# Strassen weight sums made together, and one normalised operand moved to another tile, in an encoder trunk

## The chip, the cores and the metric

The kernel runs on one core of a Trainium2 chip. The metric is the time on the device in microseconds (us), lower is better. A time is the median of several executions.

## The reference

One layer of a bidirectional encoder on 16 learned meta tokens and 1024 tokens of width 1024, all in float32: a gated feed-forward layer, a mixer of three attention branches, a second gated feed-forward layer, each after an RMS norm, and a last norm. The change touches the two feed-forward layers:

```python
def rms_norm(x, g):
    xf = x.astype(jnp.float32)
    y = xf * lax.rsqrt(jnp.mean(xf * xf, axis=-1, keepdims=True) + EPS)
    return (y * g.astype(jnp.float32)).astype(x.dtype)

def swiglu(x, w_in, w_out):
    g, u = jnp.split(x @ w_in, 2, axis=-1)
    return (jax.nn.silu(g) * u) @ w_out
...
    h = h + 0.5 * swiglu(rms_norm(h, norm_ffn1[l]), w_ffn1_in[l], w_ffn1_out[l])
    h = h + token_mixer(...)
    h = h + 0.5 * swiglu(rms_norm(h, norm_ffn2[l]), w_ffn2_in[l], w_ffn2_out[l])
    return rms_norm(h, final_norm)[:, N_META:]
```

`w_in` is 1024 x 5632, `w_out` 2816 x 1024.

## The kernel before, in words

**Precision.** A float32 product is made of three TensorE passes. Each operand is split in two parts: ScalarE copies it to a rounded type (`copy_r`, line 96: `wH` of weights, `bh` of activations), VectorE subtracts the copy from the original (`sub`, line 99: `wL`, `bl`), and the passes are H x H, H x L and L x H (lines 495, 496 and 498). `wsplit` (line 114) does it for weights. Its tiles `wH` and `wL` have four buffers, so splits run ahead of the products.

**Strassen stations.** A feed-forward layer runs as `ffn_in` (line 506) and `ffn_out` (line 565), both as loops over *stations*: one station multiplies a 2 x 2 arrangement of weight blocks `a11`, `a12`, `a21`, `a22` with a 2 x 2 arrangement of activation blocks by the seven products of the Strassen-Winograd scheme instead of eight. `ffn_in` has 22 steps `j`: `j` = 0 runs as eight plain products (`plain`, line 441), the other 21 as stations. `ffn_out` has 12 stations. With two layers that is 66 stations.

`station` (line 461) loads the four weight blocks into two tiles, `ra` (`a11` and `a12`) and `rb` (`a21` and `a22`), each with one buffer (line 433, DMAs of line 438 on SP's queue), and makes sums of them on GpSimd: `s1` = `a21` + `a22` (line 469), `s2` = `s1` - `a11` (line 470), and `a11` - `a21`, written over `a21` (line 471). The fourth sum, `a12` - `s2`, is made inside `mats`: after product 2's split of `s2` it is written over `s2` (line 477). `products` (line 481) asks `mats` for one split after the other, in the order of `CHAIN` (line 354): products 0, 1, 2, 4, 3, 6, 5. Product 6 takes the fourth sum. Each product runs for two blocks of columns, `b` = 0 and 1, into PSUM banks that are taken in turn (`psd`, line 89), and is then added up by VectorE (line 504) or copied by ScalarE.

**Operand builds.** For `ffn_in`, `build_b` (line 377) prepares the seven right-hand operands of a block. Four multiplications each (line 398, VectorE) make `b11`, `b21`, `b12` and `b22`, which are split at once as operands 0, 1, 3 and 6 (`final`, line 387) and used by `j` = 0. Then come four differences `t1` to `t4` (lines 409 to 412; on GpSimd by line 102 in the first layer, on VectorE by line 99 in the second), written over tiles that are no longer needed, and the splits of operands 2, 4 and 5, later of operand 3. `b11`, `b12` and `b21` lie in the tiles `oA`, `oT` and `e` of the block; `b22` and `t1` lie in the two tiles that later hold operand 5 (`slot_tags`, line 357). The tile `e` is also that of `ev` (line 530), the three evacuated pieces of a step. Tile `oA1` is also used for `wt` (line 1422), sums of the second layer's output weights, made on GpSimd by `tsums` (line 369, lines 372 to 375), as are sums of activations (`tsum`, line 627), which go to DRAM by stores of lines 631 to 633.

**What sets the order.** The program is written in one order, and a scheduler of the tile framework orders each engine's queue ahead of time with a timing simulation of its own (`schedule_with_timeline_sim=True`); so an instruction can stand elsewhere in its queue than in the text. On the chip each queue runs in its written order, and an instruction that waits holds up all behind it on its engine. A tile with one buffer is reused when the last reader of its old content is done.

Of the kernel before, what the change touches and what calls it, by code (L numbers as in the profile page):

```python
# [9 lines left out]
F32 = mybir.dt.float32  # L10
F32R = mybir.dt.float32r
AF = mybir.ActivationFunctionType
ALU = mybir.AluOpType

P = 128
# [20 lines left out]
class Trunk:  # L36
# [61 lines left out]
    def sub(self, out, a, b):  # L98
        return self.nc.vector.tensor_tensor(out=out, in0=a, in1=b, op=ALU.subtract)  # L99
# [20 lines left out]

    def dense(self, ps, W, XH, XL, c0, n, nk=KT):
        mm = self.nc.tensor.matmul
        order = self.KORD if nk == KT else range(nk)
        for i, k in enumerate(order):
            H, L = W[k // 4]
            ks = slice(k % 4 * P, (k % 4 + 1) * P)
            mm(ps[:, :n], H[:, ks], XH[k][:, c0:c0 + n], start=(i == 0), stop=False)  # L127
            mm(ps[:, :n], H[:, ks], XL[k][:, c0:c0 + n], start=False, stop=False)  # L128
            mm(ps[:, :n], L[:, ks], XH[k][:, c0:c0 + n], start=False, stop=(i == nk - 1))  # L129
# [3 lines left out]

    def ahead(self, W, col, chunks, tags):

        for (c0, n), tag in zip(chunks, tags):
            self.pre[col, c0] = ps = self.ps(tag)
            self.dense(ps, W, self.uh, self.ul, c0, n)

    def proj(self, box, col, c0, n):  # L140
        ps = self.pre.pop((col, c0), None)
        if ps is None:
            ps = self.dps()
            self.dense(ps, box["W"], self.uh, self.ul, c0, n)
        return ps

    def wfirst(self, col):
        W = self.W0.pop(col, None)
        return self.wcols(self.w_in, col, self.sub_pool) if W is None else W
# [227 lines left out]
    def build_b(self, pool, bt, w, blk, h, gcol, c0, tags, sub, ordered):  # L377


        nc = self.nc  # L380
        n = 4 * w
        b11, b12, b21 = (pool.tile([P, n], F32, tag=tag, name="bu") for tag in tags)
        p5, th, tl = self.slot_tags(pool, blk, 5)
        b22, t1 = (p5.tile([P, n], F32, tag=tag, name="bu") for tag in (th, tl))
        last = []

        def final(i, src):
            bt[blk][i] = HL = self.bslot(pool, blk, i, w)
            return self.split_b(HL, src)

        def norm(q, t, i):
            hs = slice((q % 2) * w, (q % 2) * w + w)
            rs = slice(c0 + hs.start, c0 + hs.stop)

            with self.behind(last[-2] if ordered and len(last) > 1 else None):
                for kk in range(4):
                    k = kk + 4 * (q // 2)
                    nc.vector.scalar_tensor_tensor(
                        out=t[:, kk * w:(kk + 1) * w], in0=h[:, k, hs], scalar=self.gT[:, gcol + k:gcol + k + 1],
                        in1=self.R[:, rs], op0=ALU.mult, op1=ALU.mult)  # L400
            last.append(final(i, t))

        norm(0, b11, 0)
        norm(2, b21, 1)
        yield
        norm(1, b12, 3)
        norm(3, b22, 6)
        t2, t3, t4 = b11, b12, b21
        sub(t1, b12, b11)
        sub(t2, b22, t1)  # L410
        sub(t3, b22, b12)
        sub(t4, b21, t2)
        for i, src in ((2, t2), (4, t1), (5, t4)):
            final(i, src)
        yield
        final(3, t3)
        yield
# [43 lines left out]
    def station(self, pool, srcs, nk=4):  # L461

        nc = self.nc
        n = nk * P
        a11, a12, a21, a22 = self.raws(pool, srcs, n)
        s1 = pool.tile([P, 512], F32, tag="s1", name="s1")[:, :n]
        s2 = pool.tile([P, 512], F32, tag="s2", name="s2")[:, :n]
        tt = nc.gpsimd.tensor_tensor
        tt(out=s1, in0=a21, in1=a22, op=ALU.add)  # L469
        tt(out=s2, in0=s1, in1=a11, op=ALU.subtract)  # L470
        tt(out=a21, in0=a11, in1=a21, op=ALU.subtract)

        def mats(i):
            src = (a11, a12, s2, a21, s1, a22, s2)[i]
            W = self.wsplit(src)
            if i == 2:
                tt(out=s2, in0=a12, in1=s2, op=ALU.subtract)
            return W
        return mats

    def products(self, mats, bts, w, nk, evac, after=None):
# [106 lines left out]
    def ffn1(self, hT):  # L588
# [3 lines left out]
        with tc.tile_pool(name="f1", bufs=1, reuse_waits="tile") as pool:  # L592
# [6 lines left out]
            def block(b, lead):  # L599
                for i in ([] if b else [8]) + list(range(4 * b, 4 * b + 4)):  # L600
                    self.load_x(pool, hT, i)[1]()
                steps = self.build_b(pool, bt, w, b, hT[:, :, 2 * w * b:2 * w * (b + 1)], 0, 2 * w * b,
                                     (f"oA{b}", f"oT{b}", f"e{b}"), self.sub_pool, False)
                next(steps)
                next(steps)
                if b == 0:
                    lead()
                for _ in range(4):
                    yield
                next(steps)  # L610
                yield
# [26 lines left out]
            def after(i):  # L638
                for b in range(2):
                    nxt[b][i] = build(0, b, i, 4)  # L640

            self.ffn_in(pool, a["w_ffn1_in"][0], bt, w, block, emit, after)
            def srcs(c, n, nk):
                rows = w1o[8 * c * P:(8 * c + 2 * nk) * P, :].rearrange("(k i p) d -> i p k d", i=2, p=P)
# [730 lines left out]
    def ffn2(self, hp):  # L1375
# [3 lines left out]
        with tc.tile_pool(name="f2", bufs=1, reuse_waits="tile") as pool:  # L1379
# [6 lines left out]
            def block(b, lead):  # L1386
                if b == 0:
                    lead()
                steps = self.build_b(pool, bt, w, b, hT[:, :, 512 * b:512 * b + 512], 16, NM + 512 * b,
                                     (f"oA{b}", f"oT{b}", f"e{b}"), self.sub, True)  # L1390
                next(steps)
                next(steps)
                yield
                yield
                for f in ([] if b else self.token_half(pool, ssum, 1)):
                    pin = f()
                    yield pin
                if b:
                    yield
                    yield  # L1400
                next(steps)
                yield
# [32 lines left out]
            def after(i):  # L1435
                for b in range(2):
                    nxt[b][i] = build(0, b, i, 4)

            self.ffn_in(pool, a["w_ffn2_in"][0], bt, w, block, emit, after)
            hacc = hp.tile([P, 8, D], F32, tag="h", name="hacc")  # L1440
            for i in range(8):
# [112 lines left out]
```

## Time and profile before

| | before |
|---|---|
| median of 3 executions | 2679.34 us |
| lowest and highest | 2678.97, 2684.99 us |
| the profiled execution | 2684.01 us |
| its span, first to last instruction | 2682.2 us |
| mean granted TensorE clock | 0.987 |
| busy: TensorE, VectorE, ScalarE, GpSimd | 96%, 62%, 48%, 30% |

PE is TensorE's matmuls, PEld its weight loads, DVE VectorE, ACT ScalarE, POOL GpSimd, SP SyncE, which issues DMAs. A `q` after the engine's name marks its sequencer. A row of a timeline has the start, the duration, the engine, the line, the operation, the tiles (out<-in), the shape and the count; in brackets stands how long the engine had been idle before it, and what ended that.

### The profile page before, as it was taken

How to read it: one execution, taken by the hardware profiler on the slowest of the kernel's cores; microseconds unless marked ns; L12 is line 12 of the kernel's file. 1: busy time of each engine (PE TensorE's matmuls, PEld its weight loads, DVE VectorE, ACT ScalarE, POOL GpSimd, SP SyncE). 2: the span in 40 equal slices, each digit the busy share in tenths (PEclk: the TensorE clock that was granted, in tenths of full speed). 3: DMA queues.
4: the chain of work that ended last, by engine and by line, in shares of the span. 5: the costliest groups of instructions: out<-in, count | busy, mean ns of one | idle time of the engine just before them, and what ended most of it. 6: DMA issues, size and time to landing. Idle time of an engine off the chain costs nothing.

```text
span 2682.2 us, 46662 instructions
## 1 busy us (share of the span) xinstructions
PE 2587.5 (96%) x17648; PEld 2384.7 (89%) x17648; DVE 1664.3 (62%) x3569; ACT 1283.5 (48%) x2456; POOL 807.0 (30%) x697
## 2 busy tenths in 40 slices
PE   6999999999999999999999999999999999999998
PEld 5999999899989989999998888788789999998786
DVE  7644455766867767866777444645485444447667
ACT  5433333532446655656677555554344334334333
POOL 5443454523411111122221111004104444443322
PEclk8999999999999999999999999999999999999999
DMA  3244632542431222223322332436434545566433
GB/s 100 78 126 123 201 112 88 208 134 87 162 108 58 73 71 76 54 70 76 79 62 70 94 93 89 133 99 199 131 99 142 171 154 157 182 228 204 157 122 102
DMA packets 366576, 319.90 MB, mean 119 GB/s; under 512 B 33880, under 2 KB 323759, under 8 KB 366350
## 3 DMA queue, kind: packets, MB, share of 16 engines
q1 hardware_dynamic: 357420, 311.96, 37.6%
q10 hardware_dynamic: 8498, 4.21, 0.6%
q8 instruction: 139, 2.28, 0.4%
q0 software_dynamic: 432, 0.74, 0.2%
q14 instruction: 87, 0.71, 0.1%
HBM read 220.39 MB, written 94.78 MB: 118 GB/s over the span
## 4 chain that ended last, share of the span: by engine, by line
PE 76%; DVE 7%; DMA 6%; issue 5%; POOL 3%; ACT 3%; SPq 0%; POOLq 0%; DVEq 0%; ACTq 0%
PE ps_d L127 7%; PE ps_d L128 7%; PE ps_d L129 7%; PE ps_s L495 5%; PE ps_s L496 5%; PE ps_s L498 5%; PE ps_t L495 5%; PE ps_t L496 5%; PE ps_t L498 5%; PE ps_t L854 3%; PE ps_s L842 2%; PE ps_s L843 2%; PE ps_d L495 2%; PE ps_d L496 2%; PE ps_d L498 2%
## 5 line engine op out<-in xcount | busy, mean ns | idle before, releaser
L127 PE MATMUL ps_d<-uh,wH 128*128 128x512 f32 (+2 forms) x1096 | 381.7, 348 | 6.0 <-DVE t L832 3.2
L129 PE MATMUL ps_d<-uh,wL 128*128 128x512 f32 (+2 forms) x1096 | 375.7, 343 | 0.0
L128 PE MATMUL ps_d<-ul,wH 128*128 128x512 f32 (+2 forms) x1096 | 375.6, 343 | 0.0
L495 PE MATMUL ps_s<-bh,wH 128*128 128x260 f32 (+2 forms) x1229 | 328.5, 296 | 14.5 <-ACT wH L96 9.2
L495 PE MATMUL ps_t<-bh,wH 128*128 128x260 f32 (+2 forms) x1225 | 326.3, 295 | 5.8 <-ACT ev L532 2.1
L102 POOL TENSOR_TENSOR wL<-wr,wH 128x512 fp32r<-128x512 f32 x104 | 134.6, 1305 | 641.9 <-ACT wH L96 423.3
L496 PE MATMUL ps_s<-bl,wH 128*128 128x260 f32 (+2 forms) x1229 | 326.7, 294 | 0.0
L496 PE MATMUL ps_t<-bl,wH 128*128 128x260 f32 (+2 forms) x1225 | 325.3, 294 | 0.0
L469 POOL TENSOR_TENSOR s<-rb 128x512 f32<-128x512 f32 (+1 forms) x66 | 91.6, 1388 | 622.6 <-DMA rb<-in_w_ffn_in_dram 275.2
L495 PEld LDWEIGHTS ps_s<-bh,wH 128*128 128x128 f32 x1229 | 232.6, 189 | 24.6 <-ACT wH L96 10.9
L495 PEld LDWEIGHTS ps_t<-bh,wH 128*128 128x128 f32 x1225 | 232.7, 190 | 14.8 <-ACT wH L96 4.1
L99 DVE TENSOR_TENSOR pL<-ps_t,pH 128x256 fp32r<-128x256 f32 (+2 forms) x264 | 151.9, 582 | 140.5 <-ACT pH L96 130.6
L496 PEld LDWEIGHTS ps_s<-bl,wH 128*128 128x128 f32 x1229 | 232.8, 189 | 6.0 <-issue 0.9
L496 PEld LDWEIGHTS ps_t<-bl,wH 128*128 128x128 f32 x1225 | 232.4, 190 | 5.9 <-issue 0.9
L127 PEld LDWEIGHTS ps_d<-uh,wH 128*128 128x128 f32 x1096 | 207.2, 189 | 30.4 <-DVE t L832 4.4
L96 ACT ACTIVATE wH<-s 128x512 fp32r<-128x512 f32 (+1 forms) x198 | 120.7, 616 | 231.5 <-POOL s L470 102.3
L129 PEld LDWEIGHTS ps_d<-uh,wL 128*128 128x128 f32 x1096 | 207.3, 189 | 23.3
L128 PEld LDWEIGHTS ps_d<-ul,wH 128*128 128x128 f32 x1096 | 207.4, 189 | 19.7
L99 DVE TENSOR_TENSOR wL<-s,wH 128x512 fp32r<-128x512 f32 (+1 forms) x198 | 171.2, 866 | 76.4 <-ACT wH L96 75.9
L498 PE MATMUL ps_s<-bh,wL 128*128 128x260 f32 (+2 forms) x1229 | 212.4, 294 | 0.0
L498 PE MATMUL ps_t<-bh,wL 128*128 128x260 f32 (+2 forms) x1225 | 210.9, 293 | 1.3 <-DVE wL L99 1.3
L96 ACT ACTIVATE pH<-ps_t 128x256 fp32r<-128x256 f32 (+2 forms) x264 | 130.1, 508 | 124.2 <-PE ps_o L938 34.5
(372 smaller groups left out, 6614.9 us busy)
## 6 DMA issues: line engine op xcount, KB each, us to landing
ra<-in_w_ffn_in_dram SPq DMA_DIRECT2D x88, 256.0 KB
rb<-in_w_ffn_in_dram SPq DMA_DIRECT2D x88, 256.0 KB
bl<-optd SPq DMA_DIRECT2D x35, 512.0 KB
wr<-in_w_in_dram SPq DMA_DIRECT2D x30, 512.0 KB
bl<-opd SPq DMA_DIRECT2D x28, 520.0 KB
q<-q SPq DMA_DIRECT2D x48, 256.0 KB
wr<-in_w_gate_dram SPq DMA_DIRECT2D x24, 512.0 KB
gd<-t SPq DMA_DIRECT2D x48, 256.0 KB
```

What stands on the lines that cost most here:

```text
L96: self.nc.scalar.activation(out, in_, AF.Copy, scale=scale)
L99: return self.nc.vector.tensor_tensor(out=out, in0=a, in1=b, op=ALU.subtract)
L102: self.nc.gpsimd.tensor_tensor(out=out, in0=a, in1=b, op=ALU.subtract)
L127: mm(ps[:, :n], H[:, ks], XH[k][:, c0:c0 + n], start=(i == 0), stop=False)
L128: mm(ps[:, :n], H[:, ks], XL[k][:, c0:c0 + n], start=False, stop=False)
L129: mm(ps[:, :n], L[:, ks], XH[k][:, c0:c0 + n], start=False, stop=(i == nk - 1))
L469: tt(out=s1, in0=a21, in1=a22, op=ALU.add)
L495: mm(ps, H[:, ks], bH[:, cs], start=(begins and x == 0), stop=False, skip_group_check=not begins)
L496: mm(ps, H[:, ks], bL[:, cs], start=False, stop=False, skip_group_check=not begins)
L498: mm(ps, L[:, ks], bH[:, cs], start=False, stop=(x == nk - 1), skip_group_check=not begins)
L842: mm(ps[:, :n], T[:, s, 0, qs], k[:, ks:ks + n], start=True, stop=False)
L854: nc.tensor.transpose(pt[:rows, i * P:(i + 1) * P], src, self.ident)
```

## The change

The fourth weight sum gets a tile of its own (`s4`, tag `s3`), is made right after `s2`, and `mats` only splits. In `build_b`, `b21` moves from the tile `e` of the block to the first of the two tiles of operand 2; `t4` is made before `t3`, and operand 2 is split after 4 and 5. The tile `e` thereby holds only `ev` (and in the second layer `res` of the output projection), three quarters of its former size.

```diff
@@ build_b
-        b11, b12, b21 = (pool.tile([P, n], F32, tag=tag, name="bu") for tag in tags)
+        b11, b12 = (pool.tile([P, n], F32, tag=tag, name="bu") for tag in tags)
         p5, th, tl = self.slot_tags(pool, blk, 5)
         b22, t1 = (p5.tile([P, n], F32, tag=tag, name="bu") for tag in (th, tl))
+        p2, th, _ = self.slot_tags(pool, blk, 2)
+        b21 = p2.tile([P, n], F32, tag=th, name="bu")
...
         sub(t1, b12, b11)
         sub(t2, b22, t1)
+        sub(t4, b21, t2)
         sub(t3, b22, b12)
-        sub(t4, b21, t2)
-        for i, src in ((2, t2), (4, t1), (5, t4)):
+        for i, src in ((4, t1), (5, t4), (2, t2)):
             final(i, src)
@@ station
         tt = nc.gpsimd.tensor_tensor
+        s4 = pool.tile([P, 512], F32, tag="s3", name="s4")[:, :n]
         tt(out=s1, in0=a21, in1=a22, op=ALU.add)
         tt(out=s2, in0=s1, in1=a11, op=ALU.subtract)
+        tt(out=s4, in0=a12, in1=s2, op=ALU.subtract)
         tt(out=a21, in0=a11, in1=a21, op=ALU.subtract)
 
         def mats(i):
-            src = (a11, a12, s2, a21, s1, a22, s2)[i]
-            W = self.wsplit(src)
-            if i == 2:
-                tt(out=s2, in0=a12, in1=s2, op=ALU.subtract)
-            return W
+            return self.wsplit((a11, a12, s2, a21, s1, a22, s4)[i])
         return mats
@@ both calls of build_b (ffn1 and ffn2)
-                                     (f"oA{b}", f"oT{b}", f"e{b}"), ...
+                                     (f"oA{b}", f"oT{b}"), ...
```

## Rows read from the trace of the kernel before

**Rows 1.** The page, part 1: busy us, share of the span, instructions.
```profile
PE 2587.5 (96%) x17648; PEld 2384.7 (89%) x17648; DVE 1664.3 (62%) x3569; ACT 1283.5 (48%) x2456; POOL 807.0 (30%) x697
```
**Rows 2.** Stretches: us, busy us (count) per engine, granted clock, DMA share, GB/s.
```profile
2030.00:2380.00 350.00, 350.00 (x2960) 350.00 (x2959) 169.54 (x294) 138.21 (x275) 147.35 (x136) 1.00 0.52 161
...
526.80:532.10 5.30, 0.18 (x2) 0.00 (x0) 5.30 (x7) 4.02 (x5) 2.87 (x2) 0.73 0.57 176
532.10:536.00 3.90, 3.90 (x18) 3.90 (x19) 2.97 (x6) 0.02 (x1) 0.00 (x0) 0.50 0.24 74
```
**Rows 3.** Line 477 in the whole trace: durations, and what ended GpSimd's idle time.
```profile
L477 POOL TENSOR_TENSOR s<-ra,s x66: 1013/1292/1741, 77.4 to 2658.6; 128x512 f32<-128x512 f32 x58, 128x384 f32<-128x384 f32 x8
...
  DVE wL L99: 55.3, 51
```
**Rows 4.** Timeline of GpSimd, 510 to 531 us.
```profile
517.40 2.28 POOL L471 TENSOR_TENSOR rb<-ra,rb 128x512 f32<-128x512 f32 x1
...
521.69 1.20 POOL L375 TENSOR_TENSOR tsum<-act,tsum 128x260 f32<-128x260 f32 x1
...
526.25 1.72 POOL L477 TENSOR_TENSOR s<-ra,s 128x512 f32<-128x512 f32 x1
```
**Rows 5.** Timeline of SP's queue, 516 to 531 us.
```profile
522.91 0.36 SPq L633 DMA_DIRECT2D opd<-tsum  x1
527.99 0.93 SPq L438 DMA_DIRECT2D ra<-in_w_ffn_out_dram  x2
```
**Rows 6.** Timeline of ScalarE, 520 to 533 us.
```profile
528.00 0.63 ACT L96 ACTIVATE wH<-s 128x512 fp32r<-128x512 f32 x1 [5.00 <-POOL s L477]
...
531.44 0.61 ACT L96 ACTIVATE wH<-ra 128x512 fp32r<-128x512 f32 x1
```
**Rows 7.** Timeline of TensorE, 526 to 536 us.
```profile
532.11 0.58 PE L495 MATMUL ps_s<-bh,wH 128*128 128x260 f32 x1 [5.12 <-ACT wH L96]
```
**Rows 8.** Timeline of TensorE, 2018 to 2022 us.
```profile
2021.54 0.39 PE L495 MATMUL ps_t<-bh,wH 128*128 128x256 f32 x1 [2.12 <-ACT ev L532]
```
**Rows 9.** Timeline of ScalarE, 2014 to 2022 us.
```profile
2020.58 0.63 ACT L96 ACTIVATE wH<-s 128x512 fp32r<-128x512 f32 x1 [5.13 <-POOL s L477]
2021.12 0.36 ACT L532 ACTIVATE ev<-ps_t 128x256 f32<-128x256 f32 x1
```
**Rows 10.** Timeline of GpSimd, 2011 to 2024 us.
```profile
2014.04 4.60 POOL L372 TENSOR_TENSOR wt<-wo 128x256 f32<-128x256 f32 x1 [20.53 <-DVE bl L99]
...
2019.29 1.26 POOL L477 TENSOR_TENSOR s<-ra,s 128x512 f32<-128x512 f32 x1
```
**Rows 11.** Timelines of ScalarE, 2449 to 2456 and 2536 to 2541 us.
```profile
2451.32 0.63 ACT L96 ACTIVATE wH<-s 128x512 fp32r<-128x512 f32 x1 [0.36 <-POOL s L477]
...
2538.72 1.06 ACT L96 ACTIVATE bh<-bl 128x1024 fp32r<-128x1024 f32 x1 [0.42 <-DMA bl<-optd]
```
**Rows 12.** Timelines of TensorE around 2455, 2540 and 2619 us.
```profile
2455.89 0.50 PE L495 MATMUL ps_s<-bh,wH 128*128 128x512 f32 x1 [1.71 <-ACT wH L96]
...
2540.35 0.79 PE L495 MATMUL ps_d<-bh,wH 128*128 128x512 f32 x1 [3.66 <-ACT wH L96]
...
2619.40 0.51 PE L495 MATMUL ps_s<-bh,wH 128*128 128x512 f32 x1 [1.03 <-ACT wH L96]
```
**Rows 13.** Timeline of GpSimd, 2605 to 2616 us.
```profile
2613.29 1.02 POOL L477 TENSOR_TENSOR s<-ra,s 128x384 f32<-128x384 f32 x1 [3.29 <-ACT bh L96]
```
**Rows 14.** Timelines of GpSimd, 24 to 46 and 56 to 73 us.
```profile
37.03 1.30 POOL L471 TENSOR_TENSOR rb<-ra,rb 128x512 f32<-128x512 f32 x1
...
56.54 16.02 POOL L102 TENSOR_TENSOR bu<-bu 128x1040 f32<-128x1040 f32 x4 [2.82 <-issue]
```
**Rows 15.** Timeline of VectorE, 61 to 76 us.
```profile
64.43 5.86 DVE L99 TENSOR_TENSOR bl<-bu,bh 128x1040 fp32r<-128x1040 f32 x2 [3.42 <-ACT bh L96]
70.21 2.90 DVE L99 TENSOR_TENSOR wL<-ra,wH 128x512 fp32r<-128x512 f32 x1
```
**Rows 16.** Timeline of TensorE, 72 to 75 us.
```profile
73.16 0.75 PE L498 MATMUL ps_t<-bh,wL 128*128 128x260 f32 x4 [1.31 <-DVE wL L99]
```

More of the change, by code (lines that the diff above doesn't have):

```diff
@@ L602, in block @@
                 steps = self.build_b(pool, bt, w, b, hT[:, :, 2 * w * b:2 * w * (b + 1)], 0, 2 * w * b,
-                                     (f"oA{b}", f"oT{b}", f"e{b}"), self.sub_pool, False)
+                                     (f"oA{b}", f"oT{b}"), self.sub_pool, False)
                 next(steps)
@@ L1389, in block @@
                 steps = self.build_b(pool, bt, w, b, hT[:, :, 512 * b:512 * b + 512], 16, NM + 512 * b,
-                                     (f"oA{b}", f"oT{b}", f"e{b}"), self.sub, True)
+                                     (f"oA{b}", f"oT{b}"), self.sub, True)
                 next(steps)
```

## The prediction

> **What bounds the kernel now.** I read the busy shares first. TensorE is busy for 96% of the span, every other engine for 62% or less [rows 1], so a change outside TensorE can only win what TensorE spends idle or at a low clock. The table of stretches then shows where there is nothing to win: from 2030 to 2380 us, some eighteen stations of the second `ffn_in`, TensorE is busy for 350.00 of 350.00 us with 2960 matmuls, 0.118 us each, at full clock [rows 2]. The same table shows a hole at the change from the first `ffn_in` to `ffn_out`: 5.3 us almost empty, then 3.90 us at a granted clock of 0.50, the lower of TensorE's two levels, 1.2 GHz, in which 18 matmuls take 0.217 us each [rows 2].
>
> Next I asked for line 477, the fourth sum. It runs 66 times, once per station, 1.29 us in the median, and GpSimd stood idle 55.3 us in 51 of these for VectorE's `wL` of product 2 [rows 3]: the old sum overwrites the tile that this split reads. That idle time is GpSimd's and costs nothing by itself. So the question is at which stations a late line 477 reaches TensorE. Going through TensorE's gaps and what ended them, I find five places, all at the edges of the stages, and the startup.
>
> **Part 1: the fourth sum moves ahead of `mats`.** Nothing is added or removed: 66 sums of 1.29 us before and after. Moved are the sum itself, the release of `ra` (line 477 was the last reader of `a12`), the DMAs of the next `ra` on SP, and the sixth split on ScalarE. The new last reader of `ra` among the sums is line 471, which now runs one sum later.
>
> *End of the first `ffn_in` (place 1).* Line 471 ended at 517.40 + 2.28 = 519.68, then came `tsums`, then line 477 from 526.25 to 527.97 [rows 4]. SP issued the `ra` loads at 527.99, behind an `opd<-tsum` store of 522.91 [rows 5]. ScalarE waited 5.00 us for line 477 and split the new `ra` at 531.44 [rows 6]; TensorE, idle for 5.12 us, went on at 532.11 [rows 7]. After the change line 471 ends 1.72 later (line 477's time here), at 521.40. If the store still stands in front, it waits for line 375, which ended at 521.69 + 1.20 = 522.89 and now ends at 524.61; with 0.36 for its issue, `ra` goes out near 525.0, its split follows 531.44 - 527.99 = 3.45 later at 528.4, the matmul 0.67 after that at 529.1. Gain 3.0. The shorter hole also gives back part of the slow stretch, which lost 3.90 x (1 - 0.118/0.217) = 1.8 us; I take 0.5. Sum 3.5; the ends are 0 (another wait takes over at once) and 5.12 + 1.8 = 6.9. Next in line is VectorE, busy with operand splits there.
>
> *First station of the second `ffn_in` (place 2).* A matmul waited 2.12 us [rows 8] for the silu of line 532, which stood on ScalarE right behind a `wH<-s` that had waited 5.13 us for line 477 [rows 9]. Line 477 stood on GpSimd behind a `wt` sum of 4.60 us which itself waited for a VectorE split [rows 10]. With the sum made early this whole chain falls away: 2.1; ends 0 and 2.1.
>
> *Later edges (places 3 to 5).* At 2455.89 TensorE had waited 1.71 us for a split of `ra`, but ScalarE had no gap before it except 0.36 us for line 477: 0.4, ends 0 and 1.7 [rows 11, 12]. At 2540.35 it had waited 3.66 us; on ScalarE the gap that this could close is 0.42 us, a wait for operands: 0.4, ends 0 and 3.7 [rows 11, 12]. At 2619.40 it had waited 1.03 us; there line 477 stood idle 3.29 us, more than the whole stall: 1.0, ends 0 and 1.0 [rows 12, 13].
>
> *At nothing.* Line 471 itself comes a sum later in all stations. It feeds the fifth product, and in the full stretch TensorE never waits [rows 2]; without that cover it would cost 1.29 us a station. `tsums` behind it are later or earlier by a sum; only stores wait for them.
>
> **Part 2: `b21` in product 2's tile.** No instruction is added. `e0` and `e1` shrink by a quarter, which pays for the new tile. A wait goes: the first `ev` of a block shared its tile with `b21`, so line 532 had to follow product 5's split; I count no gain for it. A wait comes: product 2's copy may only start when product 5's split has read `t4`, so its split is now the last but one of a block. Behind it on ScalarE and VectorE stand the first weight splits. In block 1 of the first `ffn_in` four GpSimd sums take 16.02 us [rows 14]; VectorE's two operand subtracts behind them take 5.86, then the first `wL` 2.90 [rows 15], and TensorE waited 1.31 us for that `wL` [rows 16]. With product 2's subtract gone from in front of it, `wL` can start up to 2.93 earlier and the 1.31 vanish. Against that, the fourth weight sum now enters GpSimd's queue early, beside line 471 at 37.03 [rows 14], among the sums and small powers on which the startup hangs: 1.30 at that row's time. These two cancel: 0; the ends are a gain of 1.3 and a loss of 1.30 + 2.93 = 4.2. In the second `ffn_in`, the `wt` sum waits for product 2's split of block 1 and starts later; behind it there stands line 477 no more, and its results only go to a store.
>
> **A rule against it.** Line 471 took 2.28 us at place 1, where VectorE was full of operand splits [rows 4], and 1.30 at 37.03 [rows 14]; so GpSimd and VectorE do hold each other up. The Trainium skill, GPSIMD Engine Reference, section 1 (Specifications), says that GpSimd's SBUF interfaces are shared with VectorE and contend with VectorE instructions that have two SBUF inputs. By that rule the sum, pushed into the stretch full of splits, would hold VectorE for as long as it runs. In the rows' terms that is 1.72 us lost at place 1 [rows 4]: 1.8 left there, 5.7 in all, 2673.6. That time lies inside the forecast's own band; I give it 0.10 of the 0.45 below, since the same sum ran in the same stretch before, only 9 us later.
>
> **Sum.** 3.5 + 2.1 + 0.4 + 0.4 + 1.0 + 0 = 7.4 us. The profiled execution took 2684.01 us, 1.8 more than its span of 2682.2, and lies 4.7 above the median 2679.34; against it the sum gives 2676.6, against the median 2671.9. I forecast **2672 us**. All upper ends (6.9 + 2.1 + 1.7 + 3.7 + 1.0 + 1.3 = 16.7) give 2662.6, no gain and the lower end of the start give 2683.5.
>
> **Rivals.**
> *The next wait takes over.* At place 1 VectorE, at places 3 and 4 ScalarE's queue keeps TensorE waiting; or the order written into the queues puts the new sum behind `tsums` again, so that it isn't made early where it matters. For it: ScalarE's missing gaps at place 3. Against it: place 2 has a clear chain with idle ScalarE. Only about 2 us are left: 2677. Chance 0.23.
> *More than the sum.* `ra` goes out ahead of the store, the clock stays up through place 1, and the start wins 1.3: 6.9 + 2.1 + 0.4 + 0.4 + 1.0 + 1.3 = 12.1, 2667. For it: line 471 ends before that store. Chance 0.14.
> *Slower: product 2's operand comes late.* Place: the four block builds, where the copy into the shared tile waits for product 5's subtract and ScalarE's queue stands behind it. Price: one stretched subtract, 2.93 us [rows 15], each time it isn't covered; with three of four uncovered and the stations' gains lost, 2679.3 + 8.8 = 2688. It decides if TensorE reaches the third product before that split, so if the idle time before 92 us and between 2012 and 2030 us grows by over 5. Against it: the third product comes two products, some 5.7 us at 24 x 0.118 each, after the first. Chance 0.18, and it reaches from 2681 up.
> *The forecast*, 2667 to 2677: 0.45.
>
> **Numbers.** About 0.3%, 8.0 us, is what a measurement can tell from no change, so faster begins below 2671.3. The forecast lies on that line: a little over half of its 0.45 is below, 0.26, with 0.14 from the larger gain: faster 0.40. The rest, 0.19, with 0.23 and 0.03 of the slower case: same 0.45. Slower 0.15. The range from 2663 to 2685 leaves out most of the slower case above and little below.
>
> **What would show it.** Right: line 477's work stands directly behind line 470's in each station with no idle for `wL`; the hole at 527 to 536 us is half as long; no 5 us wait of ScalarE near 2020; TensorE's total idle is some 7 us less. Wrong: TensorE's wait at these places is as long, with another releaser; or the start up to the first station is longer by several us.

## The result and the profile after

The changed kernel takes 2704.99 us in the median of 4 executions (2701.66 to 2710.63), beside 2679.15 for the kernel before (4 executions now): 1.0087 of it, 95% interval 1.0071 to 1.0104. It is slower, by 23 us by that ratio and by 26 in the medians, where the prediction had 2672, and lies outside the predicted range. The profiled execution took 2701.66 us, its span is 2699.8.

The page's first part, kernel after:

```profile
PE 2593.9 (96%) x17648; PEld 2387.4 (88%) x17648; DVE 1665.7 (62%) x3569; ACT 1282.2 (47%) x2456; POOL 815.6 (30%) x697
```

Counts are those of [rows 1], shares lie within a point: no engine has more to do, so I look for gaps. Stretches of after, columns as in [rows 2]:

```profile
526.80:532.10 5.30, 5.26 (x44) 5.26 (x45) 5.30 (x7) 3.88 (x5) 5.30 (x5) 1.00 0.70 227
532.10:536.00 3.90, 2.61 (x22) 2.44 (x21) 3.90 (x5) 0.63 (x1) 0.22 (x1) 1.00 0.40 137
2030.00:2380.00 350.00, 340.96 (x2860) 338.90 (x2859) 167.31 (x285) 131.92 (x266) 148.08 (x132) 1.00 0.49 153
```

The hole of place 1 is filled but for 1.3 us, and the granted clock there is 1.00. But the second `ffn_in`, where the prediction saw nothing to win or lose, has 2860 matmuls in the 350 us that held 2960: 100 x 0.118 = 11.8 us of work pushed out of that window.

To see where the time goes I put the start of the k-th of the 17648 matmuls of each profile beside that of before (difference in us; the kernels in the other columns are the experiments below):

| k | where | before | before again | after | build_only | pin_ra | sum_f2 | sum_f1 |
|---|---|---|---|---|---|---|---|---|
| 800 | start done | 134.3 | 0.0 | +3.0 | +0.8 | +1.3 | +0.1 | +1.8 |
| 3600 | ahead of place 1 | 485.7 | -2.6 | +4.3 | +1.0 | +1.7 | -0.2 | +1.6 |
| 4000 | past place 1 | 542.5 | -1.5 | +0.1 | -2.0 | -2.3 | -3.1 | -2.4 |
| 13200 | second `ffn_in`, first stations | 2022.6 | +3.7 | 0.0 | -1.7 | -3.5 | -6.5 | -4.8 |
| 16400 | its end | 2402.3 | +4.6 | +11.4 | -3.3 | -5.9 | +9.4 | -6.9 |
| 16800 | first `ffn_out` stations | 2464.2 | +4.8 | +15.4 | -1.6 | -5.4 | +13.2 | -6.9 |
| 17647 | the last | 2673.7 | +3.3 | +17.9 | -1.8 | -3.4 | +13.2 | -9.1 |

The loss of after is 11.4 us in the loop, 4.0 at its end and 2.5 behind it; the start's 4.3 are given back at place 1. (Two executions of one and the same kernel, before and before again, are themselves up to 5.5 us apart on the way, so single microseconds of this table prove nothing.)

What waits in the loop? From the list of waits, 2030 to 2420 us, I show the lines that matter, here and below: engine and line, what for, us in total, times, longest. Before:

```profile
DVE act L1412 <- DMA actd<-act: 24.6, 16, 4.0
ACT ev L547 <- DVE act L1412: 18.7, 12, 4.2
PE ps_d L495 <- ACT ev L547: 0.7, 1, 0.7
SPq L1414 <- DVE act L1412: 116.2, 34, 9.7
SPq L438 <- POOL s L477: 13.3, 19, 2.6
```

After:

```profile
DVE act L1412 <- DMA actd<-act: 70.7, 19, 7.3
ACT ev L547 <- DVE act L1412: 57.9, 19, 5.5
PE ps_d L495 <- DVE act L1412: 7.8, 5, 3.1
PE ps_d L495 <- ACT ev L547: 3.9, 5, 1.5
SPq L1414 <- DVE act L1412: 70.1, 19, 6.9
SPq L440 <- POOL s L474: 57.4, 18, 6.2
```

In the two last lines the weight has moved: before, SP's queue stood mostly at a store of `act` (line 1414) and waited for VectorE to fill it; now it also stands at a load of `ra` (line 440) and waits for the fourth sum (now line 474), and the store stands behind. SP's order of these instructions in the traces, station by station, other DMAs left out:

```
before, every station:  actd<-act, ra x2, actd<-act, rb x2
after, one station:     ra x2, actd<-act x2, rb x2
after, the next:        ra, actd<-act, ra, actd<-act, rb x2
```

One station on the clock. Before, timelines of VectorE and SP:

```profile
2195.56 0.41 DVE L1412 SCALAR_TENSOR_TENSOR act<-ev,ps_o 128x256 f32<-128x256 f32 x1
...
2200.06 0.43 DVE L1412 SCALAR_TENSOR_TENSOR act<-ev 128x256 f32<-128x256 f32 x1 [2.03 <-DMA actd<-act]
...
2195.99 0.34 SPq L1414 DMA_DIRECT2D actd<-act  x1
2197.04 1.83 SPq L438 DMA_DIRECT2D ra<-in_w_ffn_in_dram  x2
```

After, timelines of GpSimd, SP, VectorE and ScalarE, and TensorE's longest wait of this kind, further on:

```profile
2194.58 1.29 POOL L472 TENSOR_TENSOR s<-rb 128x512 f32<-128x512 f32 x1 [11.88 <-DMA rb<-in_w_ffn_in_dram]
...
2197.64 1.29 POOL L475 TENSOR_TENSOR rb<-ra,rb 128x512 f32<-128x512 f32 x1
2198.89 1.46 POOL L474 TENSOR_TENSOR s<-ra,s 128x512 f32<-128x512 f32 x1
...
2200.38 0.92 SPq L440 DMA_DIRECT2D ra<-in_w_ffn_in_dram  x2
2201.40 7.73 SPq L1414 DMA_DIRECT2D actd<-act  x2
...
2225.68 0.37 SPq L440 DMA_DIRECT2D ra<-in_w_ffn_in_dram  x1
2226.14 0.51 SPq L1414 DMA_DIRECT2D actd<-act  x1
...
2200.83 0.41 DVE L1412 SCALAR_TENSOR_TENSOR act<-ev,ps_o 128x256 f32<-128x256 f32 x1
...
2207.73 0.70 DVE L1412 SCALAR_TENSOR_TENSOR act<-ev 128x256 f32<-128x256 f32 x1 [5.19 <-DMA actd<-act]
...
2224.42 0.41 DVE L1412 SCALAR_TENSOR_TENSOR act<-ev,ps_s 128x256 f32<-128x256 f32 x1
...
2208.85 0.37 ACT L547 COPY ev<-ps_t 128x256 f32<-128x256 f32 x1 [4.30 <-DVE act L1412]
...
2419.71 0.58 PE L495 MATMUL ps_d<-bh,wH 128*128 128x256 f32 x1 [3.07 <-DVE act L1412]
```

Before, block 0's act ends at 2195.56 + 0.41 = 2195.97, its store goes out 0.02 later, ahead of the `ra` loads, and block 1's act can start at 2200.06, 4.09 after the end. After, GpSimd has waited for `rb` until 2194.58 and makes its sums; line 474, still behind the third sum (now line 475) and so still the last reader of `ra`, ends at 2200.35, and 0.03 later SP issues the two `ra` loads of 256 KB each. The store of block 0, ready at 2201.24, goes out behind them at 2201.40: block 1's act, which waits for it, starts at 2207.73, 6.49 after the end. In the next station the store is held on SP besides: ready at 2224.83, issued at 2226.14, 1.31 later. In the six stations between 2130 and 2250 us it takes 2.2 to 4.4 us from block 0's act to block 1's before, 4.6 to 6.5 after. `act` has one buffer, and the act of a block reads a PSUM bank and the tile `ev`. So while it is held, that bank stays taken, ScalarE's copy into `ev` of the next station stands behind (4.30 us here), and TensorE waits for both: 7.8 and 3.9 us in the list above.

### The profile page after: what moved, and what is told of

The parts are those of the page before. It is cut to its first block, busy times and chain, and to the rows that moved or that the text cites. A ratio compares the mean times of both kernels' runs of the same rounds, so it can differ in the third digit from the quotient of the medians.

```text
span 2699.8 us, 46667 instructions
## 1 busy us (share of the span) xinstructions
PE 2593.9 (96%) x17648; PEld 2387.4 (88%) x17648; DVE 1665.7 (62%) x3569; ACT 1282.2 (47%) x2456; POOL 815.6 (30%) x697
## 5 line engine op out<-in xcount | busy, mean ns | idle before, releaser
L99 DVE TENSOR_TENSOR wL<-s,wH 128x512 fp32r<-128x512 f32 (+1 forms) x198 | 182.4, 924 | 70.2 <-ACT wH L96 69.8
```

## The experiments

**Theory.** The early sum moved the `ra` loads ahead of the act stores in SP's queue; the stores go out and land later, and the single `act` tile passes the delay on to TensorE. **Rival 1:** the operand build (Part 2) makes product 2 late. **Rival 2:** GpSimd, with three sums in a row, or VectorE beside it, is what holds the loop. Eleven runs; the median of before is 2682.35 us for the first four, 2682.72 for the next four and 2682.11 for the last three.

| run | median us | of before, 95% interval |
|---|---|---|
| build_only | 2683.52 | 1.0000 [0.9990, 1.0009] |
| pin_ra | 2683.44 | 1.0006 [0.9997, 1.0016] |
| act_two | 2684.57 | 1.0011 [1.0001, 1.0020] |
| act_actq | 2694.26 | 1.0044 [1.0028, 1.0059] |
| before_again | 2687.38 | one execution |
| sum_f2 | 2698.60 | 1.0057 [1.0040, 1.0074] |
| sum_f1 | 2679.13 | 0.9983 [0.9974, 0.9992] |
| pin_in | 2685.90 | 1.0008 [0.9995, 1.0021] |
| sum_f1_again | 2676.32 | 0.9977 [0.9964, 0.9991] |
| sum_in1 | 2681.48 | 1.0003 [0.9989, 1.0017] |
| sum_f1_t3 | 2676.01 | 0.9981 [0.9970, 0.9992] |

**build_only: the station as before, the operand build as changed.**

```diff
-        tt(out=s4, in0=a12, in1=s2, op=ALU.subtract)
...
+            if i == 2:
+                tt(out=s2, in0=a12, in1=s2, op=ALU.subtract)
```

> The changed kernel with its station as it was before (fourth sum after product 2's split, in the place of s2); the operand build with b21 in product 2's tile stays. Theory (SP queue order: the early sum moves the ra loads ahead of the act stores in the second ffn_in): SP's order in that loop is a store before each load again, so the loop's 11.4 us are gone: TensorE busy 350 of 350 us there. The loss of the start-up (4.3 us) stays, the gain of place 1 (4.2 us) goes: 2683 us, 2680 to 2688. Rival 1 (product 2 late through the operand build): the build is all there, so 2700 to 2710. Rival 2 (the three sums together and the wt sums press on GpSimd and VectorE): 2680 to 2688 as well, told apart by the next two.

Measured 1.0000. The stretch 2030 to 2400 us of this run:

```profile
2030.00:2400.00 370.00, 369.48 (x3134) 369.23 (x3133) 176.39 (x310) 143.72 (x288) 156.88 (x146) 1.00 0.54 171
```

The loss is gone with the early sum alone undone; rival 1 falls. The start is 0.8 us late at matmul 800 and 1.0 at 3600, where after is 3.0 and 4.3: the loss at the start, expected to stay, has mostly gone too.

**sum_f2: the early sum in the second `ffn_in` alone, on the kernel before.** Its tile is taken from another pool, since there was no room for it beside the old operand build; in the first block the sum alone, without the new build, wasn't run.

```diff
+        early = self.second is not None and ffn_in
+        s4 = self.second.tile([P, 512], F32, tag="ssum", name="s4")[:, :n] if early else s2
...
+        if early:
+            tt(out=s4, in0=a12, in1=s2, op=ALU.subtract)
```

> The kernel before with one part of the change alone, in one place: in the second ffn_in loop the fourth sum has its own tile and is made with the other three; the operand build, the first ffn block and both ffn_out stages stay as they were. SP's written order in that loop is then that of the changed kernel (ra loads ahead of the act stores), with nothing of the operand build in it. Theory (the early sum moves SP's order): the loop loses some 11 us and its end up to 4 more, the start loses nothing: 1.004 to 1.006 of before, 2691 to 2698 us at a before of 2682. Rival 1 (operand build): 2679 to 2685.

Measured 1.0057, 15.9 us. The stretch:

```profile
2030.00:2400.00 370.00, 358.35 (x2987) 355.67 (x2986) 173.42 (x298) 138.92 (x280) 157.57 (x140) 1.00 0.49 154
```

The waits from 2030 to 2420 us:

```profile
DVE act L1418 <- DMA actd<-act: 67.3, 18, 7.4
ACT ev L552 <- DVE act L1418: 57.9, 18, 5.6
```

SP's timeline:

```profile
2195.89 0.92 SPq L438 DMA_DIRECT2D ra<-in_w_ffn_in_dram  x2
2196.90 7.62 SPq L1420 DMA_DIRECT2D actd<-act  x2
```

The same order and waits as in the changed kernel, and in this profile a loss of 15.9 us between matmuls 13200 and 16400, with nothing of the operand build. From 2030 to 2400 us TensorE, VectorE, ScalarE and GpSimd run their instructions in the order of before; SP's order alone is another. One moved sum in one loop is enough. By the ratios the changed kernel loses some 8 us more than this one (1.0087 beside 1.0057); where that falls is open, but pin_ra gives it back too.

**pin_ra: the whole change, SP's loads held behind the act store of two stations before.**

```diff
+        with self.behind(pin):
+            a11, a12, a21, a22 = self.raws(pool, srcs, n)
...
+                mats = self.station(pool, srcs(j), pin=self.stores.get((j - 2, 0)))
```

> The changed kernel, whole, with one thing more: the ra and rb loads of a station of the ffn_in loop are put on SP's queue behind the act store of block 0 of two stations before, as they stood before the change. Theory (SP queue order): act stores are no longer held by the loads, VectorE's waits for the DMA actd<-act fall from 70.7 us to about the 24.6 of before, TensorE is busy 350 of 350 us in 2030 to 2380, and the time falls by the 11.4 us of the loop and perhaps by the 4 at its end: 2690 to 2694 us. Rival 1 (operand build) and rival 2 (the early sums press on GpSimd): both are untouched by SP's order, 2702 to 2708.

Measured 1.0006, some 21 us below the changed kernel. The stretch:

```profile
2030.00:2400.00 370.00, 369.94 (x3139) 369.74 (x3138) 187.40 (x310) 145.09 (x287) 168.16 (x148) 1.00 0.56 173
```

The waits from 2030 to 2420 us:

```profile
DVE act L1415 <- DMA actd<-act: 56.6, 18, 4.4
ACT ev L550 <- DVE act L1415: 24.3, 19, 2.5
```

SP's timeline:

```profile
2192.61 0.34 SPq L1417 DMA_DIRECT2D actd<-act  x1
2193.13 2.04 SPq L440 DMA_DIRECT2D ra<-in_w_ffn_in_dram  x2
2197.36 0.34 SPq L1417 DMA_DIRECT2D actd<-act  x1
```

With the early sum in place and SP's order restored TensorE is full again: rival 2 falls. (Beside after, ScalarE and GpSimd keep their order in the whole trace; VectorE takes one weight split per station later, 30 of TensorE's matmuls trade places.) Two numbers of the expectation missed. The waits for the store fell to 56.6 us and not to 24.6; what fell is the longest, from 7.3 to 4.4, and waits up to that length are covered. And the time fell by more than 15 us, since the losses behind the loop went too.

**act_two: the changed order, but block 1's act in a tile of its own.**

```diff
-                o = acts[b] = pool.tile([P, 512], F32, tag="oA0", name="act")
+                o = acts[b] = (hp.tile([P, 512], F32, tag="ssum", name="act") if b else
+                               pool.tile([P, 512], F32, tag="oA0", name="act"))
```

> The changed kernel with SP's order as the change has it, but block 1's act has a tile of its own, so that it doesn't wait for block 0's store. Theory (SP queue order, passed on by the single act tile): the stores are as late as in the changed kernel, but nobody waits for them: the waits of VectorE's act for the DMA actd<-act fall to under 15 us, TensorE's waits for VectorE's act in 2030 to 2420 (7.8 us) go, 2690 to 2695 us. If the late ra or rb themselves, or GpSimd, hold the loop (rival 2): 2700 to 2706. Rival 1: 2702 to 2708.

Measured 1.0011. The stretch:

```profile
2030.00:2400.00 370.00, 369.75 (x3137) 369.55 (x3136) 193.08 (x313) 142.90 (x288) 161.11 (x144) 1.00 0.53 171
```

The waits from 2030 to 2420 us:

```profile
ACT ev L547 <- DVE act L1413: 3.4, 2, 2.9
...
SPq L440 <- POOL s L474: 60.7, 19, 6.9
```

SP's order up to 2390 us is that of after, and it still stands 60.7 us at line 440 for the sum, but no line names the DMA `actd<-act` as a wait of VectorE any more. So the late store does its harm through the one buffer of `act`. The kernel lies below the 2690 to 2695 expected, as pin_ra does.

**act_actq: the act stores on ScalarE's queue.**

```diff
-                nc.sync.dma_start(out=self.actd[j, :, 512 * b:512 * b + 512], in_=o)
+                nc.scalar.dma_start(out=self.actd[j, :, 512 * b:512 * b + 512], in_=o)
```

> The changed kernel with the act stores issued on ScalarE's DMA queue and not on SP's. Theory (SP queue order): the loads at SP's head hold nothing that VectorE waits for, so 2690 to 2696 us; ScalarE's issue waits for VectorE's act and may delay the evictions behind it by up to 1 us a block (32 blocks and more, most of it hidden), upper end 2700. Rivals 1 and 2: 2702 to 2710.

Measured 1.0044, within the theory's band but only half of the loss back. Most of this profile's loss, 7.1 us, comes at the end of the loop (matmuls 16400 to 16800). A new wait of 2030 to 2420 us may stand for the rest; no run isolates it:

```profile
DVE act L1412 <- DMA actd<-act: 20.8, 12, 5.4
ACT wH L96 <- DVE act L1412: 20.4, 7, 4.7
```

ScalarE now waits for VectorE's act in order to issue the store, with weight splits behind it. A wait was moved from one queue to another.

**before_again: the kernel before, profiled once more.** No edit.

> The kernel before, unaltered, profiled a second time, to tell how far one execution's waits differ from another's. If the waits that the prediction priced (5.1 us at the end of the first ffn_in loop, 2.1 us at the second loop's first station) are set by the order of the sums, both stand again within 1 us; if they come and go between executions, the gains read at those places from the other profiles (3 to 4 us in three kernels, the early sum in them or not) are no effect of the change. The loop from 2030 to 2400: TensorE busy without a gap again.

Both waits stand again: at place 1 the longest is 3.6 us (5.12 in [rows 7]), at place 2 it is 2.7 (2.12 in [rows 8]). Place 2 has 0.6 us of play. Place 1 has more than the 1.5 seen here: build_only and sum_f2 pass it with every queue in the order of before, and there the longest wait for the split is 2.30 and 1.30 us.

**sum_f1: the early sum in the first ffn block alone; the operand build as changed.**

```diff
+        early = not self.second
+        s4 = pool.tile([P, 512], F32, tag="s3", name="s4")[:, :n] if early else s2
...
+            if i == 2 and not early:
+                tt(out=s4, in0=a12, in1=s2, op=ALU.subtract)
```

> The changed kernel with the early sum in the first ffn block alone, the station of the second block as before; the operand build stays changed. Theory: no loss in the second loop; the gain at the end of the first ffn_in loop (by the profiles 3 to 4 us, of which the operand build alone already showed 3) against a start-up loss of 1 to 3 us: 2680 to 2684 at a before of 2682, 0.999 to 1.001. If the prediction's 3.5 us of that place were real and its price of the start nothing, 2678 to 2679.

Measured 0.9983, and in **sum_f1_again**, the same file on other draws:

> The kernel of the run sum_f1 a second time (early sum in the first ffn block alone, station of the second block as before), to see whether its 0.9983 [0.9974, 0.9992] stands on another draw: if it is an effect, 0.997 to 0.999 again with an interval below 1; if it was the draw, 0.9995 to 1.001.

0.9977, interval below 1 again. This version is faster than both kernels, than the one before by 3.6 and 5.8 us in the medians, some 0.2%.

**pin_in: pin_ra with the early sum in the `ffn_in` loops alone.** Edit: `early = ffn_in` in the station.

> The changed kernel with SP's loads held behind the act stores, as in the run before with that hold, and the early sum in the two ffn_in loops alone: in the ffn_out stages, where the profiles of the changed kernel and of the held one show waits some 2 us longer at 2540 and 2640 than before, the station is as before. If the early sum is what costs there: 2 us below the held kernel, 2680 to 2682, 0.999 to 1.000 of before. If those waits come and go by themselves: as the held kernel, 2683 to 2684.

Measured 1.0008: no gain. In its profile the waits at 2530 to 2645 us are shorter (3.6 and 1.4 us at longest, 5.0 and 2.9 in pin_ra), but the time doesn't show it; its mixer, like that of sum_in1 below, is slower.

**sum_in1: sum_f1 with the early sum in the first `ffn_in` loop alone.** Edit: `early = ffn_in and not self.second`.

> As sum_f1, but the early sum in the first ffn_in loop alone; both ffn_out stages and the second loop as before. The prediction's gain of 3.5 us stands at the end of that loop: if it is what sum_f1 gains, it is all here, 0.9975 to 0.999 of before. If sum_f1's gain comes from the first ffn_out's stations, 0.9995 to 1.0005, as with the operand build alone.

Measured 1.0003: by the expectation's second case, sum_f1's gain needs the first `ffn_out`'s stations too. Its profile shows where they matter: it gains as much at place 1 and falls behind sum_f1 only in the mixer, where no station runs. From matmul 10000 to 10800 (1396 to 1526 us in before) the seven profiles with the early sum in the first `ffn_out` (after, pin_ra, act_two, act_actq, sum_f1, sum_f1_again, sum_f1_t3) take 126.7 to 127.0 us, those in the order of before (before, before_again, build_only, sum_f2) 128.7 to 131.2, sum_in1 and pin_in 131.7 and 131.8. The mixer's code is one and the same, but its instructions stand in three different orders in these three groups. So what the early sum in the first `ffn_out` brings is, as far as these profiles show, another order of the mixer; no wait that the prediction priced is in it.

**sum_f1_t3: sum_f1 with the order of t3 and t4 as before.**

```diff
+        sub(t3, b22, b12)
         sub(t4, b21, t2)
-        sub(t3, b22, b12)
```

> As sum_f1, with the operand build's t3 again before its t4, as before the change (b21 still in product 2's tile): product 3's operand is the third that the block's first products need, t4 only the first station. If the change's order there costs at the start (matmul 400 comes 0.7 to 1.8 us later in the profiles with the changed build, 0.1 without), up to 1.5 us come back: 0.997 to 0.9985 of before. If the start is set by something else (the split of b21's own operand later on ScalarE and VectorE): as sum_f1.

Measured 0.9981, as sum_f1; matmul 800 comes 3.0 us later than before. The order of these two has no price that shows.

## Why the prediction was wrong

**The step that failed** stands under "At nothing". Among what moves, the prediction named "the DMAs of the next `ra` on SP", but asked for SP's order at place 1 alone; for the other stations it relied on TensorE's full 350 us [rows 2]. That cover was worth what stood in SP's queue: it held because act stores stood ahead of the loads. The early sum took away the wait for VectorE's `wL` in front of the last reader of `ra` [rows 3], the queue was written anew, and the loads came to stand in front. What was priced at 0 measured 15.9 us in sum_f2; restoring SP's order gives 21 us back. A premise failed with it: the prediction had the third sum (line 471) run one sum later and become the last reader of `ra`. In all 66 stations of after the third sum still runs ahead of the fourth, which stays the last reader; what went is its wait. That the ordering simulation took `ra` to be free before the store's data was there is argued, not shown; on the chip the sums waited for `rb`, and `ra` came free at about the time of the store's data (2200.35 beside 2201.24).

**The slower rival** had the sign but the wrong place. It put the loss at the four block builds; build_only, with all of Part 2, is at 1.0000. Part 2's own price of 0 stands: 0.8 us at matmul 800 in one profile, nothing in the time.

**Place 1** was predicted at 3.5. From matmul 3600 to 4000 before takes 56.8 us, after 52.6: 4.2 less, more than the sum's 3.5. Part of that is luck: before_again (57.9), build_only (53.8) and sum_f2 (53.9) run this place in the order of before, and the last two gain some 3 us with the fourth sum in its old place. In sum_f2 the sum still keeps ScalarE waiting, and yet TensorE waits only 1.30 us:

```profile
526.27 0.63 ACT L96 ACTIVATE wH<-s 128x512 fp32r<-128x512 f32 x1 [3.00 <-POOL s L482]
...
530.75 0.39 PE L500 MATMUL ps_s<-bh,wH 128*128 128x260 f32 x1 [1.30 <-ACT wH L96]
```

So the 5.12 us [rows 7] that the prediction priced were the longest of four waits in one order: 5.12, 3.62, 2.30, 1.30. In the nine profiles with the early sum there this wait is gone and one for VectorE takes over, 1.96 to 2.95 us, as the first rival had it. In after:

```profile
525.62 0.74 PE L498 MATMUL ps_s<-bh,wL 128*128 128x260 f32 x4 [2.07 <-DVE wL L99]
```

These nine take 52.1 to 54.3 us for the stretch, 53.0 in the mean beside 55.6 of the four: a gain of some 2.6 us. The 1.72 us that the rule against it would lose here are told apart by no run.

**Place 2**, predicted at 2.1: the wait is gone in after (2010 to 2030 us: TensorE 20.00 of 20.00). It is gone in build_only and in sum_f2 as well, so either part alone removes it, and crediting it to the early sum was not safe.

**Places 3 to 5** were predicted at 1.8 together. At place 3 the wait of 1.71 us is gone in after, with one of 1.30 for VectorE near it. At places 4 and 5, where TensorE had waited 3.66 and 1.03 us [rows 12], it waited 4.65 and 2.87 in after:

```profile
2557.38 0.80 PE L495 MATMUL ps_d<-bh,wH 128*128 128x512 f32 x1 [4.65 <-ACT wH L96]
...
2637.99 0.79 PE L495 MATMUL ps_s<-bh,wH 128*128 128x512 f32 x1 [2.87 <-ACT wH L96]
```

Place 4 proves nothing, since build_only and sum_f2 with the old station there wait 4.13 and 4.37. Place 5 is a loss where 1.0 was to be gained: 2.87 to 3.69 us in the four profiles with the early sum in that stage, 0.74 to 1.38 in the nine without.

**The signs named beforehand.** "No idle for `wL`" in front of the fourth sum came true: GpSimd's 55.3 us of it [rows 3] have no line any more in after's list of line 474, which runs 66 times:

```profile
L474 POOL TENSOR_TENSOR s<-ra,s x66: 1017/1478/2270, 45.3 to 2676.2; 128x512 f32<-128x512 f32 x58, 128x384 f32<-128x384 f32 x8
```

That half of the sign holds; the other, line 477's work directly behind line 470's, holds in none of the 66 stations, since the third sum stands between. TensorE's total idle, to fall by some 7 us, rose from 94.7 to 105.9 (span less busy time), and none of the signs of being wrong pointed at the loop.

The sum's median grew from 1.29 to 1.48 us, 66 x 0.19 = 12 us on an engine 30% busy; with pin_ra at 1.0006 that is not what the loss hangs on. The Trainium skill, GPSIMD Engine Reference, section 1 (Specifications), tells of contention between GpSimd and VectorE; the longer median agrees with it, though no run here separates it.

The whole gain of 7.4 us was therefore not there to be had in this form: with SP's order restored (pin_ra) the time is that of before. What can be had is what sum_f1 gains, and in the profiles some 2 to 4 us of that lie in the mixer's order, at which nobody aimed.

## What to carry to other kernels

A full engine is no proof that a moved instruction is free there: ask for each queue that the move rewrites which instruction will stand at its head, what it waits for, and what stands behind it. A transfer whose tile a sum releases moves with that sum; if a store that frees a single buffer shares its queue, hold the load behind the store, or give the buffer a second tile (pin_ra and act_two: 21 and 20 us back in the medians). Where queues are ordered by a program, an edit can change the order far from itself (here the mixer's) and leave other stretches alone: compare the orders, and try the parts of an edit apart, as sum_f1 does. And price no wait from one profile: that of place 1 was 5.12, 3.62, 2.30 and 1.30 us in four executions of one order.

## What was not expected of the hardware

A 256 KB store of `act` issued 1.02 us behind two 256 KB loads let its tile go only 6.3 us later (2201.40 to 2207.73); ahead of them, it took 4.1 (2195.99 to 2200.06). The Trainium skill, DMA: Bandwidth & Descriptors, section Queues, rings and completion order, says that each DMA engine takes the descriptors of one queue's ring in their order; these two times agree with it, and so does act_actq, where the store left SP's ring and VectorE's waits for it fell from 70.7 us to 20.8. In the six stations named above a store let the tile go 3.5 to 6.3 us after its issue in after, 2.2 to 4.4 before. Waits of VectorE for that store up to 4.4 us each, 56.6 us in all, cost TensorE nothing; at up to 7.3 us each, 70.7 in all, the loop lost 11.4. And executions of one unchanged kernel spread widely here: the 25 of before beside the first four runs lie between 2674.36 and 2688.45, so a gain of 4 us took a dozen executions or more of either kernel to tell (sum_f1).
